# A hybrid decoder layer on one core: x's rows spaced alike, head products in runs of like matmuls, conv halves of 272 columns

## The chip, the core and the metric

One core of a Trainium2 chip runs the whole layer in one launch. TensorE (PE) multiplies: a matmul takes a 128x128 block of weights, which a separate weight load (PEld) brings in, and streams a moving operand of up to 512 columns past it into a bank of PSUM. VectorE (DVE), ScalarE (ACT) and GpSimd (POOL) do elementwise work; SyncE (SP) and POOL issue the transfers between device memory and the on-chip memory SBUF (128 partitions). The metric is the time of one execution on the device in microseconds (us).

## The reference

One layer, 512 tokens after 16 meta tokens (L = 528), model width 2048, 8 attention heads of 128, 1024 conv channels, feed-forward width 5632.

```python
h = concat([meta, x])                                  # 528 x 2048
p = rmsnorm(h, g_mix) @ w_in
q, k, v, gb, gc, u = split(p)                          # 1024 columns each
q, k = rmsnorm(q per head), rmsnorm(k per head)
o_attn = stick_breaking_attention(q, k, v)             # sigmoid gates, reverse cumulative sum of logs
o_conv = gb * causal_dwconv3(gc * u, conv_w)           # y_t = sum of w[i] * (gc*u)_{t-2+i}
o = concat([rmsnorm(o_attn), rmsnorm(o_conv)])
h = h + o @ w_out
h = h + (silu(n2 @ w_gate) * (n2 @ w_up)) @ w_down     # n2 = rmsnorm(h, g_ffn)
return h[16:]
```

## The kernel before

Everything is kept transposed: channels on the partitions, tokens along the free dimension. A product in near-fp32 precision is made of three matmuls per 128 channels of the contraction: a value is split into a high and a low part (`split`: ACT copies the high part, DVE subtracts it), and weights high x data high, weights high x data low, weights low x data high are summed in PSUM. Weights come in quads of eight 128x128 blocks: SP loads a quad into `w_buf` (line 172), ACT and DVE split it into `s_buf` (lines 188 and 189), two or three quads ahead of PE.

x, scaled by its gain, is held as sixteen pairs of tiles `nh0`..`nh15` (high) and `nl0`..`nl15` (low), one pair for each 128 of the 2048 channels (`split_x`). Each tile is 528 floats long, 2112 bytes of a partition, and they lie one behind the other. The list of them is `n_hl`.

The order of the work, stage by stage:

- **Start** (0 to 30 us): x arrives tile by tile; the products for k and q of head 0 (`pk0`, `pq0`) advance together in groups of 2, 2, 4, 4 and 4 tiles of x, as ACT and DVE split them.
- **Heads** (to about 345 us): for each head a product for k (`pk`), q (`pq`) and v (`pv`), `product_steps` (lines 271 to 287). k and v have 528 columns and are done in two parts of 264, one in each of two PSUM banks; for a tile of x the two parts follow each other for each of the three kinds (L280, L282, L284). q has the 512 real tokens in one part. The attention of the head before is woven in: `after(n, work)` queues a piece of work, and `tick()`, called once for each tile of x, issues it after n ticks. Attention's own matmuls are the few on lines 465 to 616.
- **First two conv channel blocks** (345 to about 415 us): products `pcu` (c and u, 520 columns in two parts of 260 that begin at token column `C0` = 8) and `pb` (b, 512 columns in one part).
- **Other six conv channel blocks** (415 to about 604 us): Winograd's form of Strassen's product, seven block products for eight (`pair_product`, `block_product`, lines 730 to 785). Its operands are halves of x's columns of width `CH` = 260, and sums of them: parts of `n_hl`, and three sums in `blk`. `form_blocks(k)` makes the sums of tiles k and k+8 during the heads: SP loads four quarters of x (`x4`), ACT scales them, DVE makes the sums, both split them, and SP stores them to `fc` in device memory. Later POOL loads three of the four kinds into `blk` (line 701) and the fourth over x's own second halves (line 708). For two channel blocks at a time `pair` is called three times: c and u of each, then b of both.
- **Output projection** (604 to 786 us, `po`), **gate and up** (786 to 1606 us, moving operands `f0`..`f6`), **down** (to the end, `first` and `ring`). In the last two every moving operand is 256 columns wide and its rows lie 1024 bytes apart; the tiles are made with `slots`, which begins each one 16 bytes into its space and pads it by 240 bytes more. In `po` the rows are 512 columns, 2048 bytes apart. None of this is touched by the change.

The tile framework orders each engine's instructions by a schedule that it computes when the program is built, and each engine runs its own in order.

Of the kernel before, what the change touches and what calls it, by code (L numbers as in the profile page):

```python
# [15 lines left out]
P = 128  # L16
D = 2048
# [16 lines left out]
def hybrid_layer(ctx: ExitStack, tc: tile.TileContext, xT, w_in, w_out, w_gu, w_down, vecs, out):  # L34
# [23 lines left out]
    sm = open_pool("sm", 4, space=PSUM)  # L58

# [211 lines left out]
    def product_steps(parts, acts, n):  # L271

        k, last = 0, n - 1
        while k <= last:
            hi, lo, m = next_w()
            for j in range(m):
                wh, wl = hi[:, j * P : (j + 1) * P], lo[:, j * P : (j + 1) * P]
                ah, al = acts[k]
                for ps, a, b in parts:
                    pe.matmul(ps, wh, ah[:, a:b], start=k == 0, stop=False)  # L280
                for ps, a, b in parts:
                    pe.matmul(ps, wh, al[:, a:b], start=False, stop=False)  # L282
                for ps, a, b in parts:
                    pe.matmul(ps, wl, ah[:, a:b], start=False, stop=k == last)  # L284
                k += 1
                tick()
            yield
# [34 lines left out]
    H = L // 2  # L322
    n_hl = []
# [6 lines left out]
    def x_scale():  # L330
        ve.tensor_tensor(acc, acc, accs[1], ALU.add)
        for a in (0, H):
            ps = small(f"ssx{a}")
            pe.matmul(ps[:, :H], ones, acc[:, a : a + H], start=True, stop=True)
            ve.tensor_scalar(ms[:, a : a + H], ps[:, :H], 1.0 / D, EPS, ALU.mult, ALU.add)
# [11 lines left out]
    def split_x(k):  # L347
        nh = npool.tile([P, L], F32R, tag=f"nh{k}", name=f"nh{k}")
        nl = npool.tile([P, L], F32R, tag=f"nl{k}", name=f"nl{k}")
        g = g_mix[:, k : k + 1]  # L350
        sc.activation(nh, xts[k], AF.Copy, scale=g)
        ve.scalar_tensor_tensor(nl, xts[k], g, nh.bitcast(F32), ALU.mult, ALU.subtract)
        n_hl.append((nh, nl))

    def square_x(k):
# [6 lines left out]

    pk0 = pp.tile([P, 2, 512], F32, tag="pp", name="pk0")
    pq0 = pp.tile([P, 2, 512], F32, tag="pp", name="pq0")
    steps = [
        product_steps([(pk0[:, 0, :H], 0, H), (pk0[:, 1, :H], H, L)], n_hl, KT),
        product_steps([(pq0[:, 0, :], META, L)], n_hl, KT),
# [43 lines left out]
    C0, CH = 8, (L - 8) // 2  # L411
    fc = dram.tile([P, 4, 2, 8, CH], F32R, name="fc")

    def form_blocks(k):

        x4 = stage.tile([P, 4, CH], F32, tag="x4", name=f"x4_{k}")
        st = stage.tile([P, 8 * CH], F32R, tag="st", name=f"st4_{k}").rearrange("p (i a t) -> p i a t", i=4, a=2)
        for i, kk in ((0, k), (2, k + 8)):
            nc.sync.dma_start(x4[:, i : i + 2], two(xT[kk][:, C0:]))
# [20 lines left out]
    def halves(ps, n):  # L440
        return ps[:, :, :n]

# [3 lines left out]
    def qk_norm(ps, g, cols, dst, parts_of, name):  # L446
# [9 lines left out]
        raw_v, s_v = (raw, s) if cols == SEQ else (two(raw), two(s))  # L456
        sc.activation(s_v, ps, AF.Square)
        sc.activation(raw_v, ps, AF.Copy, scale=g)
# [21 lines left out]
    def head(h):  # L480

        if h:
            pk = pp.tile([P, 2, 512], F32, tag="pp", name=f"pk{h}")
            product([(pk[:, 0, :H], 0, H), (pk[:, 1, :H], H, L)], n_hl)
        else:
            pk = pk0
# [3 lines left out]
        after(8 if h else 11, qk_norm(halves(pk, H), g_k, L, kn[:, :L], (kh, kl, 384), f"k{h}"))  # L490

        if h:
            pq = pp.tile([P, 2, 512], F32, tag="pp", name=f"pq{h}")
            product([(pq[:, 0, :], META, L)], n_hl)
        else:
            pq = pq0
# [3 lines left out]
        after(9 if h else 12, qk_norm(pq[:, 0, :], gq_s, SEQ, qn, (qh, ql, SEQ), f"q{h}"))  # L500

        pv = pp.tile([P, 2, 512], F32, tag="pp", name=f"pv{h}")
        product([(pv[:, 0, :H], 0, H), (pv[:, 1, :H], H, L)], n_hl)
        vt = t512(L, "e", 2)
        ve.tensor_tensor(two(vt[:, :L]), halves(pv, H), two(r), ALU.mult)
# [120 lines left out]
    for h in range(HEADS):  # L626
        if h > 1:
            after(6, lambda h=h: form_blocks(h - 2))
        head(h)
# [23 lines left out]
    def conv_taps(j, c1, c2, y):  # L653

        ve.tensor_tensor(c1, c1, two(r2[:, C0:]), ALU.mult)
        ve.tensor_tensor(c1, c2, c1, ALU.mult)
        cu = c1.rearrange("p a b -> p (a b)")
        o = META - 2 - C0
        sc.activation(y, cu[:, o : o + SEQ], AF.Copy, scale=cw[:, 3 * j : 3 * j + 1])
        for t in (1, 2):  # L660
            ve.scalar_tensor_tensor(
                y, cu[:, o + t : o + t + SEQ], cw[:, 3 * j + t : 3 * j + t + 1], y, ALU.mult, ALU.add
            )
# [12 lines left out]
    for j in range(CONV_FIRST):  # L676
        if j == 0:
            after(2, lambda: form_blocks(6))
            after(12, lambda: form_blocks(7))
        c1, c2 = halves_of("e"), halves_of("e2")  # L680
        for c in (c1, c2):
            p = pp.tile([P, 2, 512], F32, tag="pp", name="pcu")
            product([(p[:, 0, :CH], C0, C0 + CH), (p[:, 1, :CH], C0 + CH, L)], n_hl)
            sc.copy(two(c), halves(p, CH))
# [3 lines left out]
        product([(pb[:, 0, :], META, L)], n_hl)  # L688
        gb = t512(SEQ, "e2", 2)[:, :SEQ]
        sc.copy(gb, pb[:, 0, :])  # L690
        if j == 0:
# [6 lines left out]
            blk = blk_pool.tile([P, 3, 2, 8, CH], F32R, name="blk")  # L698
            for i, n in enumerate((3, 0, 2)):
                for part in range(2):  # L700
                    gp.dma_start(blk[:, i, part], fc[:, n, part], max_dma_last_dim=4160)
# [4 lines left out]
    for k in range(8):  # L706
        for part in range(2):
            gp.dma_start(n_hl[k][part][:, C0 + CH :], fc[:, 1, part, k])

    def parts_of(kk, a):  # L710
        return lambda part, k: n_hl[kk + k][part][:, a : a + CH]

    def of_blk(i):
        return lambda part, k: blk[:, i, part, k]

    conv_acts = [
        parts_of(0, C0), of_blk(0), of_blk(1), of_blk(2), parts_of(0, C0 + CH), parts_of(8, C0), parts_of(8, C0 + CH)
# [69 lines left out]
    def pair(acts):  # L787
        c1, c2 = halves_of("e"), halves_of("e2")
# [4 lines left out]
    for j in range(CONV_FIRST, HEADS, 2):  # L793
        ys = []
        for m in range(2):
            c1, c2 = pair(conv_acts)
# [17 lines left out]
        for m in range(2):  # L814
            s = t512(SEQ, "e", 2)[:, :SEQ] if j == HEADS - 2 else cpool.tile([P, SEQ], F32, tag="s", name=f"sq{j}_{m}")
            with tc.high_priority(1 << 20) if j == HEADS - 2 else ExitStack():
                conv_out(j + m, gbs[m][:, META - C0 :], ys[m], slots[m][:, 0], slots[m][:, 1], s, ve)
# [43 lines left out]

    def pad(pool, n):
        pool.tile([P, n // 4], F32, name=f"pad_{pool.name}")
# [372 lines left out]
```

## Time and profile before

| | |
|---|---|
| median of 3 runs | 2040.07 us (2039.51 to 2040.22) |
| the profiled execution: its own time | 2039.67 us |
| its span, from first to last instruction | 2038.0 us |
| DVE busy | 1718.7 us (84%) |
| ACT busy | 1049.0 us (51%) |
| POOL busy | 379.9 us (19%) |
| DMA queue of SP / of POOL | 229.51 MB, 35.5% / 129.65 MB, 24.2% of 16 engines' span |

A row of the timeline gives the start in us, how long it took, the engine, the line, the operation, output<-inputs, partitions x columns, and a count where rows were merged. TensorE's matmuls overlap: the next one begins long before the one before has left the array, so what counts for the time is the distance from start to start, called pitch below, and not the duration in the row.

### The profile page before, as it was taken

Reading aid. Unit: us, or ns where it says so; the run is one execution under the profiler, and the core shown is the slowest. Engines: PE = TensorE matmul, PEld = TensorE weight load, DVE = VectorE, ACT = ScalarE, POOL = GpSimd, SP = SyncE. Lnnn points to the kernel's source line nnn. Section 1 sums busy time; section 2 is a strip of 40 time slices with the busy share of each in tenths; the row PEclk is TensorE's granted clock in tenths of the full one; section 3 lists DMA queues with packets and bytes.
Section 4 is the critical chain, followed back from the end, with each engine's and each line's share of the span. In section 5 each row is a group of like instructions: output and inputs, shape, how many; then the busy total and the mean of one; then the engine's idle time right before and its main releaser. Section 6 shows DMA issues by size and latency. Waiting matters only on the chain.

```text
span 2038.0 us, 39734 instructions
## 1 busy us (share of the span) xinstructions
PE 2028.5 (100%) x16158; PEld 1964.8 (96%) x16158; DVE 1718.7 (84%) x2202; ACT 1049.0 (51%) x1517; POOL 379.9 (19%) x532
## 2 busy tenths in 40 slices
PE   9999999999999999999999999999999999999999
PEld 8999999999998889999999999999999999999999
DVE  8788878588877678998988988988989988888887
ACT  7666666344443435554554554555555544444443
POOL 0111111210015440101111111110110252222111
PEclk9999999999999999999999999999999999999999
DMA  6333344753365656556555555555555999989864
GB/s 231 111 119 124 124 136 130 253 150 104 104 212 181 187 175 231 155 169 174 159 165 158 159 161 161 158 161 158 163 160 155 278 312 310 243 236 262 228 154 89
DMA packets 161863, 361.70 MB, mean 177 GB/s; under 512 B 13584, under 2 KB 73488, under 8 KB 161680
## 3 DMA queue, kind: packets, MB, share of 16 engines
q1 hardware_dynamic: 79744, 229.51, 35.5%
q0 software_dynamic: 81936, 129.65, 24.2%
q8 instruction: 127, 2.08, 0.4%
q14 instruction: 56, 0.46, 0.1%
HBM read 278.50 MB, written 80.61 MB: 176 GB/s over the span
## 4 chain that ended last, share of the span: by engine, by line
PE 93%; DVE 3%; ACT 2%; issue 1%; DMA 1%; POOL 0%; DVEq 0%; POOLq 0%; ACTq 0%
PE x L742 13%; PE x L744 13%; PE x L743 13%; PE z L742 6%; PE z L743 6%; PE z L744 6%; PE y L742 3%; PE y L743 3%; PE y L744 3%; PE po L843 3%; PE po L845 3%; PE po L844 3%; PE pv L280 2%; PE pv L284 1%; PE pv L282 1%
## 5 line engine op out<-in xcount | busy, mean ns | idle before, releaser
L188 ACT CAST s_buf<-w_buf 128x1024 fp32r<-128x1024 f32 (+2 forms) x665 | 659.3, 991 | 764.7 <-PE x L743 341.1
L189 DVE TENSOR_TENSOR s_buf<-w_buf,s_buf 128x1024 fp32r<-128x1024 f32 (+2 forms) x665 | 767.2, 1154 | 174.4 <-ACT s_buf L188 174.1
L742 PE MATMUL x<-f,s_buf 128*128 128x256 f32 x1408 | 387.7, 275 | 0.6 <-ACT sides L772 0.5
L744 PE MATMUL x<-f,s_buf 128*128 128x256 f32 x1408 | 387.2, 275 | 0.0
L743 PE MATMUL x<-f,s_buf 128*128 128x256 f32 x1408 | 387.2, 275 | 0.0
L201 DVE TENSOR_TENSOR w_buf<-w_buf 128x1024 f32<-128x1024 f32 (+1 forms) x243 | 277.5, 1142 | 14.7 <-DMA w_buf<-w_in 10.4
L742 PEld LDWEIGHTS x<-f,s_buf 128*128 128x128 f32 x1408 | 264.3, 188 | 1.4 <-ACT sides L772 0.9
L743 PEld LDWEIGHTS x<-f,s_buf 128*128 128x128 f32 x1408 | 264.3, 188 | 0.0
L744 PEld LDWEIGHTS x<-f,s_buf 128*128 128x128 f32 x1408 | 264.3, 188 | 0.0
L1038 POOL DMA_DIRECT2D fd<-s x147 | 103.6, 921 | 705.0 <-DVE s L295 703.7
L742 PE MATMUL z<-f,s_buf 128*128 128x256 f32 x704 | 193.6, 275 | 0.0
L743 PE MATMUL z<-f,s_buf 128*128 128x256 f32 x704 | 193.6, 275 | 0.0
L744 PE MATMUL z<-f,s_buf 128*128 128x256 f32 x704 | 193.6, 275 | 0.0
L744 PE MATMUL x<-ring,s_buf 128*128 128x256 f32 x608 | 167.3, 275 | 1.0 <-DVE s_buf L189 1.0
L742 PE MATMUL x<-ring,s_buf 128*128 128x256 f32 x608 | 167.2, 275 | 0.0
L743 PE MATMUL x<-ring,s_buf 128*128 128x256 f32 x608 | 167.2, 275 | 0.0
L742 PEld LDWEIGHTS z<-f,s_buf 128*128 128x128 f32 x704 | 132.1, 188 | 0.0
L744 PEld LDWEIGHTS z<-f,s_buf 128*128 128x128 f32 x704 | 132.1, 188 | 0.0
L743 PEld LDWEIGHTS z<-f,s_buf 128*128 128x128 f32 x704 | 132.1, 188 | 0.0
L1108 POOL DMA_DIRECT2D out_T<-d x62 | 60.2, 1001 | 302.7 <-DVE d L1116 232.3
L744 PEld LDWEIGHTS x<-ring,s_buf 128*128 128x128 f32 x608 | 114.1, 188 | 1.2 <-DVE s_buf L189 1.2
L742 PEld LDWEIGHTS x<-ring,s_buf 128*128 128x128 f32 x608 | 114.1, 188 | 0.0
(379 smaller groups left out, 5252.3 us busy)
## 6 DMA issues: line engine op xcount, KB each, us to landing
w_buf<-w_gu SPq DMA_DIRECT2D x176, 512.0 KB, 3.4
w_buf<-w_in SPq DMA_DIRECT2D x92, 512.0 KB, 3.4
fd<-s POOLq DMA_DIRECT2D x147, 256.0 KB, 5.2
w_buf<-w_down SPq DMA_DIRECT2D x96, 384.0 KB, 4.9
ring<-fd POOLq DMA_DIRECT2D x42, 768.0 KB, 8.7
w_buf<-w_out SPq DMA_DIRECT2D x32, 512.0 KB, 3.6
out_T<-d POOLq DMA_DIRECT2D x62, 256.0 KB, 5.4
fc<-st SPq DMA_DIRECT2D x8, 1040.0 KB, 6.2
```

Source lines behind the costliest of these rows:

```text
L188: sc.copy(hi, src)
L189: in_turn(ve.tensor_tensor(lo, src, hi.bitcast(F32), ALU.subtract), turn)
L201: in_turn(ve.tensor_tensor(sums[name], a, b, ALU.add), turn)
L280: pe.matmul(ps, wh, ah[:, a:b], start=k == 0, stop=False)
L742: pe.matmul(p, hi[:, kk], act(0, k), start=start and j == k == 0, stop=False, skip_group_check=skip)
L743: pe.matmul(p, hi[:, kk], act(1, k), start=False, stop=False, skip_group_check=skip)
L744: pe.matmul(p, lo[:, kk], act(0, k), start=False, stop=k == n - 1, skip_group_check=skip)
L843: pe.matmul(ps, hi[:, kk], ah, start=k == order[0], stop=False)
L844: pe.matmul(ps, hi[:, kk], al, start=False, stop=False)
L845: pe.matmul(ps, lo[:, kk], ah, start=False, stop=k == order[-1])
L1038: gp.dma_start(fd[c][s][:, :, k], t[:, :, i])
L1108: gp.dma_start(two(out[j]), c, accum_op=ALU.add)
```

## The change

It has five pieces.

1. The high and low part of a tile of x become one tile `n{k}` of 2 x 576 floats; the low part lies 2304 bytes behind the high one, and the next tile 4608 bytes further. Both distances are multiples of 256 bytes. The used row begins 12 floats in and may be 544 long (528 are x's).
2. `product_steps` turns its loops: the parts are now outside and the eight tiles of a quad inside, and a part's three kinds of matmul stay together. `H` becomes 272 (META + 256), so 528 columns are 272 + 256; q and b, 512 columns in one part before, become 256 + 256. `row_of` places the two parts one behind the other across the border of two PSUM banks.
3. The conv's halves `CH` become 272 columns wide, from token column 0 and from 256; the two halves overlap by 16 columns. The pair for b needs only 256 (`last_of` takes the last 256 of each half). `blk` gets rows of 288 floats, so that POOL's load into it has pieces of 272 floats (1088 bytes) where two long ones of 1040 floats were.
4. x's quarters for `form_blocks` are loaded by a `load_x4` of its own, queued at another tick, and in four transfers of 272 columns for two of 520.
5. The descriptor space of POOL's transfers is halved (`dynamic_dma_scratch_size=8192`), which makes room for the longer rows. The square in `conv_out` is written over b's buffer where a tile of its own was.

```diff
-            for j in range(m):
+            for i, ((ps, a, b), j) in enumerate((part, j) for part in parts for j in range(m)):
                 wh, wl = hi[:, j * P : (j + 1) * P], lo[:, j * P : (j + 1) * P]
-                ah, al = acts[k]
-                for ps, a, b in parts:
-                    pe.matmul(ps, wh, ah[:, a:b], start=k == 0, stop=False)
-                for ps, a, b in parts:
-                    pe.matmul(ps, wh, al[:, a:b], start=False, stop=False)
-                for ps, a, b in parts:
-                    pe.matmul(ps, wl, ah[:, a:b], start=False, stop=k == last)
-                k += 1
-                tick()
+                ah, al = acts[k + j]
+                pe.matmul(ps, wh, ah[:, a:b], start=k + j == 0, stop=False)
+                pe.matmul(ps, wh, al[:, a:b], start=False, stop=False)
+                pe.matmul(ps, wl, ah[:, a:b], start=False, stop=k + j == last)
+                if i % len(parts) == len(parts) - 1:
+                    tick()
+            k += m
...
-    H = L // 2
+    H, ROW = META + T2, 2304 // 4
...
-        nh = npool.tile([P, L], F32R, tag=f"nh{k}", name=f"nh{k}")
-        nl = npool.tile([P, L], F32R, tag=f"nl{k}", name=f"nl{k}")
+        n = npool.tile([P, 2 * ROW], F32R, tag=f"n{k}", name=f"n{k}")
+        n_row = n.rearrange("p (a t) -> p a t", a=2)[:, :, 12 : 12 + 2 * H]
+        nh, nl = (n_row[:, i, :L] for i in range(2))
...
+    def row_of(ps, a=0):
+        flat = ps.rearrange("p a b -> p (a b)")[:, 512 - H + a :]
+        return flat[:, : L - a], [(flat[:, : H - a], a, H), (flat[:, H - a : L - a], H, L)]
...
-    C0, CH = 8, (L - 8) // 2
+    CH = H
...
+    def load_x4(k):
+        blk_x[k] = x4 = stage.tile([P, 4, CH], F32, tag="x4", name=f"x4_{k}")
+        for i, kk in ((0, k), (2, k + 8)):
+            for m in range(2):
+                nc.sync.dma_start(x4[:, i + m], xT[kk][:, m * T2 : m * T2 + CH])
...
-            blk = blk_pool.tile([P, 3, 2, 8, CH], F32R, name="blk")
+            blk = blk_pool.tile([P, 8 + 48 * 288], F32R, name="blk")
+            blk = blk[:, 4 : 4 + 48 * 288].rearrange("p (i k a t) -> p i k a t", i=3, k=8, a=2)
...
-                    gp.dma_start(blk[:, i, part], fc[:, n, part], max_dma_last_dim=4160)
+                    gp.dma_start(blk[:, i, :, part, :CH], fc[:, n, part])
...
-        gbs = pair(conv_acts)
+        gbs = pair([last_of(act) for act in conv_acts], T2)
...
-    nc = bacc.Bacc("TRN2", target_bir_lowering=False, num_devices=1)
+    nc = bacc.Bacc("TRN2", target_bir_lowering=False, num_devices=1, dynamic_dma_scratch_size=8192)
```

TensorE in head 3's product for k, before (each row with x2 is the two parts):

```order
L280 MATMUL pk3_1569<-nh0_170,s_buf_112 128x264 x2
L282 MATMUL pk3_1569<-nl0_171,s_buf_112 128x264 x2
L284 MATMUL pk3_1569<-nh0_170,s_buf_112 128x264 x2
L280 MATMUL pk3_1569<-nh1_174,s_buf_112 128x264 x2
L282 MATMUL pk3_1569<-nl1_175,s_buf_112 128x264 x2
```

The same place now, the end of the first part and the beginning of the second (the number behind `n` is the tile of x, 0 to 15):

```order
L283 MATMUL pk3_1704<-n6_248,s_buf_112 128x272
L284 MATMUL pk3_1704<-n6_248,s_buf_112 128x272
L282 MATMUL pk3_1704<-n7_251,s_buf_112 128x272
L283 MATMUL pk3_1704<-n7_251,s_buf_112 128x272
L284 MATMUL pk3_1704<-n7_251,s_buf_112 128x272
L282 MATMUL pk3_1704<-n0_170,s_buf_112 128x256
L283 MATMUL pk3_1704<-n0_170,s_buf_112 128x256
```

Twenty-four matmuls of 272 columns go through the quad's eight tiles of x, and then twenty-four of 256 go through the same eight tiles again.

TensorE at the start, the first rows behind the warm-up, before (`pk0` and `pq0` are head 0's k and q):

```order
L280 MATMUL pk0_124<-nh0_170,s_buf_112 128x264 x2
L280 MATMUL pq0_125<-nh0_170,s_buf_112 128x512
L282 MATMUL pk0_124<-nl0_171,s_buf_112 128x264 x2
L284 MATMUL pk0_124<-nh0_170,s_buf_112 128x264 x2
L282 MATMUL pq0_125<-nl0_171,s_buf_112 128x512
L280 MATMUL pk0_124<-nh1_174,s_buf_112 128x264 x2
```

And now:

```order
L282 MATMUL pk0_124<-n0_170,s_buf_112 128x272
L282 MATMUL pq0_125<-n0_170,s_buf_112 128x256
L283 MATMUL pk0_124<-n0_170,s_buf_112 128x272
L284 MATMUL pk0_124<-n0_170,s_buf_112 128x272
L283 MATMUL pq0_125<-n0_170,s_buf_112 128x256
L284 MATMUL pq0_125<-n0_170,s_buf_112 128x256
L282 MATMUL pk0_124<-n1_173,s_buf_112 128x272
```

Half of tile 0's columns are done, and tile 1 is asked for, before the other half of tile 0 is touched.

SP's queue in the heads, where `x4` is loaded, before (`fc<-st` is the store of the sums made before it):

```order
L428 DMA fc_466<-st4_5_3555 1024x1x260
L419 DMA x4_6_3927<-xT 128x520 x2
L172 DMA w_buf_111<-w_in 128x1024 x6
L428 DMA fc_466<-st4_6_3928 1024x1x260
L419 DMA x4_7_4076<-xT 128x520 x2
L172 DMA w_buf_111<-w_in 128x1024 x3
L428 DMA fc_466<-st4_7_4077 1024x1x260
```

And now:

```order
L443 DMA fc_498<-st4_5_3889 1024x1x272
L429 DMA x4_6_4029<-xT 128x272 x4
L175 DMA w_buf_111<-w_in 128x1024 x6
L443 DMA fc_498<-st4_6_4312 1024x1x272
L429 DMA x4_7_4431<-xT 128x272 x4
L175 DMA w_buf_111<-w_in 128x1024 x2
L443 DMA fc_498<-st4_7_4463 1024x1x272
```

Between the stores the loads of x stand where they stood, right behind the store before; they are four for two, and the last store has passed one load of weights.

More of the change, by code (lines that the diff above doesn't have):

```diff
@@ L682, in hybrid_layer @@
             p = pp.tile([P, 2, 512], F32, tag="pp", name="pcu")
-            product([(p[:, 0, :CH], C0, C0 + CH), (p[:, 1, :CH], C0 + CH, L)], n_hl)
-            sc.copy(two(c), halves(p, CH))
+            row, parts = row_of(p)
+            product(parts, n_hl)
+            for m in range(2):
+                sc.copy(two(c)[:, m], row[:, m * T2 : m * T2 + CH])
         y = t512(SEQ, "v", 2)[:, :SEQ]
@@ L785, in pair_product, with pair @@
         return x
-    def pair(acts):
-        c1, c2 = halves_of("e"), halves_of("e2")
+    def pair(acts, n):
+        c1, c2 = (halves_of(t)[:, : 2 * n] for t in ("e", "e2"))
         x = pair_product(acts, two(c1), two(c2), sides)
```

78 lines of the change are left out of this document (42 added, 36 removed).

## The prediction, made before the run

> **What bounds the kernel now.** The page's busy times and its chain of waits come first.
>
> ```profile
> PE 2028.5 (100%) x16158; PEld 1964.8 (96%) x16158; DVE 1718.7 (84%) x2202; ACT 1049.0 (51%) x1517; POOL 379.9 (19%) x532
> PE 93%; DVE 3%; ACT 2%; issue 1%; DMA 1%; POOL 0%; DVEq 0%; POOLq 0%; ACTq 0%
> ```
>
> TensorE is busy throughout and is 93% of the chain, so the time is a sum of matmul pitches and a few waits. The page's "mean ns of one" can't give pitches, since matmuls overlap; a count of matmuls in a stretch without waits can. Three such stretches, from the window view (stretch, length, then busy time and count of PE, PEld, DVE, ACT and POOL, granted clock, DMA share and GB/s), and behind them the groups by shape that give one matmul's duration (the ns between the bars):
>
> ```profile
> 440.00:480.00 40.00, 40.00 (x337) 40.00 (x336) 34.99 (x39) 18.86 (x25) 0.00 (x0) 1.00 0.34 106
> 900.00:980.00 80.00, 80.00 (x708) 80.00 (x708) 72.02 (x81) 41.27 (x54) 14.46 (x21) 1.00 0.61 174
> 660.00:740.00 80.00, 80.00 (x355) 66.24 (x354) 55.56 (x77) 31.81 (x51) 36.19 (x40) 1.00 0.60 180
> L742 PE MATMUL x<-nh,s_buf 128*128 128x260 f32 x216 | 61.0, 283 | 0.5 <-ACT sides_c L772 0.5
> L744 PE MATMUL x<-f,s_buf 128*128 128x256 f32 x1408 | 387.2, 275 | 0.0
> L843 PE MATMUL po<-oa,s_buf 128*128 128x512 f32 x128 | 49.8, 389 | 0.0
> ```
>
> A count takes in matmuls that had begun before the stretch: at 283, 275 and 389 ns each and the pitches that follow, about 2.4, 2.4 and 1.7 of them.
>
> - 440 to 480, the conv's pairs, 260 columns: 40 us / 334.6 = **119.5 ns**, 0.460 ns a column.
> - 900 to 980, gate and up, 256 columns: 80 / 705.6 = **113.4 ns**, 0.443 a column.
> - 660 to 740, output projection, 512 columns: 80 / 353.3 = **226.4 ns**, 0.442 a column.
>
> Four columns more cost 6.1 ns in the first, where 0.443 each makes 1.8. So 260 columns pay 4.4 ns that 256 and 512 don't. The clock is granted in full (1.00) in all three, and DVE is busier beside the second (72.02 of 80 us) than beside the first (34.99 of 40), so neither is the reason. What differs is in the code: in the second and third every moving row begins a multiple of 256 bytes behind the last one; in the first no two neighbours do. The heads' rows, from the timeline of head 3, tell size from spacing:
>
> ```profile
> 139.87 0.40 PE L280 MATMUL pk<-nh,s_buf 128*128 128x264 f32 x2
> ...
> 142.53 0.40 PE L284 MATMUL pk<-nh,s_buf 128*128 128x264 f32 x2
> 142.76 0.39 PE L280 MATMUL pq<-nh,s_buf 128*128 128x512 f32 x1
> ...
> 145.30 0.40 PE L284 MATMUL pq<-nh,s_buf 128*128 128x512 f32 x1
> ```
>
> From 139.87 to 142.76 are 24 matmuls of 264, 120.4 ns each, 3.5 over the rate of 0.443. From 142.76 to 145.30 are 11 of 512, **230.9 ns** each where `po` has 226.4: the same size, 4.5 ns dearer, and q's rows lie 2112 bytes apart, 64 off a multiple of 256. So about 4 ns a matmul go with the spacing of the rows, whatever the size.
>
> **The change part by part.** Its own count of matmuls comes from the groups by shape, of which one row each stands here (each has two or five sisters of like count):
>
> ```profile
> L280 PE MATMUL pv<-nh,s_buf 128*128 128x264 f32 x256 | 53.0, 288 | 0.2 <-ACT tmp L458 0.2
> L280 PE MATMUL pq<-nh,s_buf 128*128 128x512 f32 x128 | 50.3, 393 | 0.0
> L280 PE MATMUL pcu<-nh,s_buf 128*128 128x260 f32 x128 | 25.8, 283 | 0.0
> L280 PE MATMUL pb<-nh,s_buf 128*128 128x512 f32 x32 | 12.7, 397 | 0.0
> ```
>
> k and v: six groups of 256 are 768 pairs of 264. q and b: 3 x 128 + 3 x 32 = 480. c and u: 3 x 128 / 2 = 192 pairs of 260. Conv pairs: 3 rounds x 3 calls x 7 products x 24 = 1512 of 260.
>
> The unknown is the pitch of 272 columns in a run. Its ends: 0.443 x 272 = 120.4 ns, if it runs as 256 and 512 do where rows are spaced alike; or what 272 columns cost now, in attention's few:
>
> ```profile
> 134.66 0.28 PE L527 MATMUL z<-qh,kh 128*128 128x272 f32 x1
> 134.78 0.29 PE L528 MATMUL z<-ql,kh 128*128 128x272 f32 x1
> 134.90 0.29 PE L529 MATMUL z<-qh,kl 128*128 128x272 f32 x1
> 135.03 0.41 PE L532 MATMUL z<-qn,kn 128*128 128x144 f32 x2
> ```
>
> That is (135.03 - 134.66) / 3 = 123.3 ns, 2.9 dearer. I take 120.4: in the new heads all 24 rows of a run begin a multiple of 256 apart (2304 and 4608 bytes), as in the 256-column run of 900 to 980, which has the same weights buffer and the same three kinds per tile; in attention weights and rows change tiles at each step.
>
> 1. k and v: a pair goes from 2 x 120.4 = 240.8 to 120.4 + 113.4 = 233.8. 768 x -7.0 = **-5.4 us**.
> 2. q and b: 230.9 to 2 x 113.4 = 226.8. 480 x -4.1 = **-2.0 us**.
> 3. c and u: 2 x 119.5 = 239.0 (528 columns for 520 now) to 233.8. 192 x -5.2 = **-1.0 us**.
> 4. Conv pairs: two calls of three take 272 columns, 1008 x (120.4 - 119.5) = +0.9 us; b's takes 256, 504 x (113.4 - 119.5) = -3.1 us. In `blk` (three products of seven, 648 matmuls) the low row lies 1152 bytes behind the high one, 128 off a multiple of 256, so two steps of three aren't alike: 432 x 4.4 (the surplus of 260 above) = +1.9 us. Bounds 0 and 648 x 4.4 = 2.9. Together **-0.3 us**.
> 5. Start. The new order asks for the low half of x's tile 7 after 10 matmuls of 272 and 10 of 256 of its group, 2.3 us, where the old one came to it after 20 of 264 and 10 of 512, 4.7 us. DVE makes that half between 16.17 and 16.93 (the first of three merged), and TensorE used it at 17.37:
>
> ```profile
> 16.17 2.12 DVE L352 SCALAR_TENSOR_TENSOR nl<-xt,vec,nh 128x528 fp32r<-128x528 f32 x3
> 17.37 0.40 PE L282 MATMUL pk<-nl,s_buf 128*128 128x264 f32 x2
> ```
>
> So there is 0.44 us of slack for 2.4 us of haste: up to +2.0 us of wait here, less what the earlier waits of the same kind have already delayed. The schedule moves ACT's squares behind the next splits, which helps. Queued behind a wait is the rest of the group and then all of TensorE. I take **+1.0 us**, between 0 and +2.0.
>
> 6. The loads of x for `form_blocks` don't move on SP's queue, as the rows of its order show. The only wait at stake is 0.8 us on TensorE where the first conv product meets head 7's attention (0.3 us before the first of these rows and 0.5 between the two, beyond a pitch):
>
> ```profile
> 364.37 0.41 PE L284 MATMUL pcu<-nh,s_buf 128*128 128x260 f32 x2
> 364.94 0.49 PE L587 MATMUL c<-sph,carry 128*128 128x512 f32 x1 [0.17 <-ACT sph L294]
> 365.65 0.50 PE L588 MATMUL c<-spl,carry 128*128 128x512 f32 x1 [0.22 <-DVE spl L295]
> ```
>
> That waits for ACT and DVE, not for a transfer. I take 0, with 0.8 either way. DVE's and ACT's wider sums (272 for 260 columns, 5%) lie beside matmuls; if that cover goes, DVE's extra is some 1 us in the heads.
>
> 7. `blk` in shorter pieces. Before, six transfers were issued and landed so:
>
> ```profile
> L701 POOL DMA_DIRECT2D blk<-fc x6: 723/733/752, 379.9 to 383.5; - x6
> DMA to landing us min/median/max: 5.8/13.1/20.9
> 390.00:395.00 5.00, 5.00 (x43) 5.00 (x43) 3.75 (x6) 1.54 (x2) 0.00 (x0) 1.00 1.10 409
> 405.00:410.00 5.00, 5.00 (x23) 4.09 (x22) 2.97 (x3) 0.00 (x0) 4.29 (x9) 1.00 1.14 280
> 410.00:415.00 5.00, 5.00 (x28) 4.25 (x27) 2.64 (x3) 2.64 (x4) 3.06 (x6) 1.00 1.14 232
> ```
>
> From 390 to 395 the engines move pieces of 4160 bytes at 409 GB/s; from 405 to 415, saturated too, pieces of 1040 bytes (L708) beside a load of weights at 280 and 232. The last of the six landed at 383.5 + 20.9 = 404.4. `blk` is 6.7 MB now; with some 2 MB of weights beside it at 232 to 280 GB/s that is 31 to 38 us from 380, until 411 to 418, and the loads over x's second halves, some 2 MB on the same queue, come behind. They are wanted by the fifth and sixth products of the first pair:
>
> ```profile
> 413.99 0.28 PE L742 MATMUL y<-nh,s_buf 128*128 128x260 f32 x1
> ```
>
> With 24 matmuls a product these begin 11.5 and 14.3 us after 413.99, and all of that some 7 us sooner by steps 1 to 5: 418 and 421. So the third of `blk` just makes it and the loads behind it may not: between 0 and +6 us. TensorE's whole queue stands behind such a wait. I take **+1.0 us**, near the end of no wait, since before `blk` was in time by 21 us (425.5 less 404.4). The halved descriptor space isn't exercised by any row; POOL is 19% busy, and what it loads for TensorE later is asked for long ahead. I take 0.
>
> Sum: -5.4 - 2.0 - 1.0 - 0.3 + 1.0 + 1.0 = **-6.7 us**. The profiled execution took 2039.67 us (1.7 more than its span), 0.4 below the median of 2040.07; that becomes 2033.0 us, and by the median 2033.4. I forecast **2033 us**.
>
> **The rivals.** (a) **272 columns stay irregular.** 272 x 4 is 64 bytes off a multiple of 256, so a row ends where the next doesn't begin. Attention's 123.3 speaks for it. 960 in the heads and 576 of the conv outside `blk` at +2.9 are +4.5 us: 2037.5.
>
> (b) **Spacing is not the cause; a matmul pays a fixed amount and its columns.** Then halving q and b costs 480 x 4 = +1.9 us, c and u +192 x 8 x 0.443 = +0.7, the wider conv 1008 x 12 x 0.443 = +5.4, b's -504 x 4 x 0.443 = -0.9; with +2.0 for steps 5 and 7, +9.1: **2049**, slower. It decides at the heads' 256 columns: 117 ns or more is this rival. Against it are the stretches with no fixed amount at all (226.4 is twice 113.4).
> The Trainium skill, TensorE: Matmul & The Clock Gate, section "Back-to-back issue gap", has such a rule: columns / 2.4 plus 2.5 ns. By its figures the same edits would be about +6 us, an estimate. By that rule 260 columns are 1.7 ns dearer than 256; the trace has 6.1, and 113.4 where the rule has 109.2, so here the measurement speaks against it.
>
> (c) **A late transfer or a longer start** at the upper ends of steps 5 and 7 takes back 3 to 6 us more of the gain: 2036 to 2039. For it: the narrow margins there. Against it: ACT and DVE are ordered anew at the start, and 232 GB/s may not be the engines' limit for such pieces.
>
> **How the numbers follow.** Forecast 0.48 (2029 to 2036), (a) 0.22, (b) 0.13, (c) 0.17. A measurement of this kernel can tell about 0.2%, 4.1 us, from no change. Faster by more (below 2036.0): nearly all of the forecast, a quarter of (a), a third of (c): 0.58. Within: the rest of (a) and (c): 0.27. Slower (above 2044.2): (b) and a little of (c): 0.15. The lower bound takes every free term at its best (no cost in `blk`, none in steps 5 and 7, the wait in 6 gone: -4.7 together), 2028; the upper one reaches through (a) and (c), which may meet, and short of (b): 2044.
>
> **What would show it.** In the new profile: the 272-column runs of `pk` and `pv` at 120 ns (272 irregular: 123 and up); the 256-column runs at 113 (b: 117); `pq` as two such runs; the conv's `blk` products dearer than those on `n` by some 3 ns a matmul; the conv's first pair without a wait for a transfer. Such a wait, on `blk` or on x's second halves 10 to 15 us into that pair, or on POOL's queue later, would speak for (c). The forecast is wrong as a whole if 256 columns in the heads don't come at 113.

## The result, and the profile after

| | before | after |
|---|---|---|
| median | 2040.14 us (2039.51 to 2041.67, 4 runs) | 2053.32 us (2050.95 to 2054.99, 4 runs) |
| the profiled execution, its span | 2039.67, 2038.0 us | 2054.32, 2052.6 us |

The changed kernel takes 1.0062 times as long, 95% interval 1.0049 to 1.0075: 13 us slower, where 7 us less was forecast and the range ended at 2044.

The page of the changed kernel, busy times and chain:

```profile
PE 2033.6 (99%) x16638; PEld 1989.1 (97%) x16638; DVE 1719.2 (84%) x2210; ACT 1053.2 (51%) x1521; POOL 383.7 (19%) x532
PE 87%; DVE 5%; ACT 3%; DMA 2%; issue 1%; SPq 1%; POOL 1%; ACTq 0%; DVEq 0%
```

TensorE's share of the chain fell from 93% to 87%, and VectorE, ScalarE and transfers took the rest: there are new waits. TensorE's waits, by the view that adds them up (who waited, for what, us in all, times, the longest one), in the changed kernel:

```profile
PE c L600 <- DVE spl L296: 5.4, 7, 1.0
PE po L866 <- DMA oc<-od_c: 1.8, 2, 1.0
...
PE c L599 <- ACT sph L295: 0.9, 1, 0.9
PE ss_k L477 <- DVE sl_k L296: 0.9, 3, 0.4
```

and what stood there before:

```profile
PE c L588 <- DVE spl L295: 0.5, 2, 0.3
...
PE c L587 <- ACT sph L294: 0.2, 1, 0.2
```

The same two waits of attention grew from 0.7 to 6.3 us. Each stage's length, from its first matmul in the timeline to the next stage's first (a second profile of the changed kernel stands beside the first, from the run changed_again below):

| us | before | after | after, again |
|---|---|---|---|
| start, to the first product for v | 30.04 | 32.18 | 34.05 |
| heads | 307.88 | 315.36 | 314.17 |
| c, u, b of two channels | 76.07 | 76.49 | 76.35 |
| six conv channels in pairs | 182.60 | 184.80 | 184.56 |
| output projection | 178.71 | 181.87 | 178.70 |
| the rest | 1262.67 | 1261.92 | 1261.90 |

Of the first profile's 14.65 us the heads lost 7.5, the output projection 3.2 (not in the second profile), the pairs 2.2, the start 2.1 (4.0 in the second). By the same lengths the heads end at 338, the pairs begin at 414 and end at 597, and the output projection ends at 775 us before the change: the 345, 604 and 786 in the list of stages above are 7 to 11 us late.

**The pitches.** A product for v in the changed kernel, the first rows of its 272-column and of its 256-column run and two later rows of the latter (start, duration, count at the end):

```profile
159.42 0.29 PE L282 MATMUL pv<-n,s_buf 128*128 128x272 f32 x1
...
162.46 0.28 PE L282 MATMUL pv<-n,s_buf 128*128 128x256 f32 x1
...
163.40 0.28 PE L284 MATMUL pv<-n,s_buf 128*128 128x256 f32 x1
...
165.10 0.28 PE L284 MATMUL pv<-n,s_buf 128*128 128x256 f32 x1
```

24 matmuls of 272 take 3.04 us, 126.7 ns each, where 120.4 was forecast. The first eight of 256 take 117.5 each, and the next fifteen 113.3: a run of 256 settles at the forecast rate, but only after some six to ten. Means over all matmuls, taken from the starts with gaps of over 60 ns left out: 272 columns 124.9 in the heads and in the pairs, 256 columns 115.0 for k and v and 114.7 for q, and in the pairs 115.4 on x's rows and 117.8 on `blk`. Other rules for what is left out move these means by up to 0.3 ns.

**The waits.** Attention works through a head's three blocks of keys from the last to the first. Between two blocks a row is carried over: VectorE adds it (`lw<-c,sp`), ScalarE makes its high part (`sph`), VectorE its low part (`spl`), and six ticks of product matmuls later TensorE needs both (`c<-sph`, `c<-spl`). VectorE in head 3 before:

```profile
153.42 0.55 DVE L593 TENSOR_TENSOR lw<-c,sp 1x400 f32<-1x400 f32 x1
153.90 0.55 DVE L596 TENSOR_TENSOR lb<-lb,c 128x400 f32<-128x400 f32 x1
154.38 0.41 DVE L426 SCALAR_TENSOR_TENSOR x<-x 128x260 f32<-128x260 f32 x1
154.72 0.68 DVE L295 TENSOR_TENSOR spl<-lw,sph 1x512 fp32r<-1x512 f32 x1
```

and after:

```profile
156.15 0.56 DVE L605 TENSOR_TENSOR lw<-c,sp 1x400 f32<-1x400 f32 x1
156.64 0.69 DVE L304 TENSOR_TENSOR tmp<-tmp 128x528 f32<-128x528 f32 x1
157.25 0.55 DVE L608 TENSOR_TENSOR lb<-lb,c 128x400 f32<-128x400 f32 x1
157.74 0.69 DVE L305 TENSOR_TENSOR tmp<-tmp,tmp 128x528 f32<-128x528 f32 x1
158.35 0.67 DVE L296 TENSOR_TENSOR spl<-lw,sph 1x512 fp32r<-1x512 f32 x1
```

Two wide steps of the norm of k (L304, L305) now stand ahead of `spl`, where one narrow step for the conv's sums stood. TensorE at the two places, before and after:

```profile
155.34 0.40 PE L587 MATMUL c<-sph,carry 128*128 128x512 f32 x1
155.58 0.39 PE L588 MATMUL c<-spl,carry 128*128 128x512 f32 x1
```

```profile
157.71 0.40 PE L599 MATMUL c<-sph,carry 128*128 128x512 f32 x1
159.08 0.50 PE L600 MATMUL c<-spl,carry 128*128 128x512 f32 x1 [0.98 <-DVE spl L296]
```

Before, `spl` ended at 154.72 + 0.68 = 155.40 and was used at 155.58: 0.2 us of slack (at the same place in the other heads it was 0.05 to 0.4). After, it ended at 159.02, and TensorE's whole queue stood. The second new delay, the store of the block sums, the loads of x behind it on SyncE, and ScalarE's first use of x; before:

```profile
133.34 0.53 SPq L428 DMA_DIRECT2D fc<-st  x1
133.91 1.29 SPq L419 DMA_DIRECT2D x<-xT  x2
...
140.25 0.73 ACT L421 ACTIVATE x<-x,vec 128x520 f32<-128x520 f32 x1 [0.45 <-DMA x<-xT]
```

and after:

```profile
136.29 0.52 SPq L443 DMA_DIRECT2D fc<-st  x1
136.87 4.14 SPq L429 DMA_DIRECT2D x<-xT  x4
...
143.43 0.75 ACT L436 ACTIVATE x<-x,vec 128x544 f32<-128x544 f32 x1 [1.41 <-DMA x<-xT]
```

Head 3 begins at 128.53 before and 130.72 after, so x is used 11.7 us into the head before and 12.7 after: the loads moved to `load_x4` did not come sooner, they came 1.0 us later, since the store ahead of them did (0.8); and issuing the four behind it took 4.14 us, where the two took 1.29. Over the heads ScalarE waited 10.1 us for x in seven waits, where it was 2.8 in six. Behind ScalarE's wait stand attention's `sph` and the squares of k (`ss_k`).

### The profile page after: what moved, and what is told of

The parts are those of the page before. It is cut to its first block, busy times and chain, and to the rows that moved or that the text cites. A ratio compares the mean times of both kernels' runs of the same rounds, so it can differ in the third digit from the quotient of the medians.

```text
span 2052.6 us, 40751 instructions
## 1 busy us (share of the span) xinstructions
PE 2033.6 (99%) x16638; PEld 1989.1 (97%) x16638; DVE 1719.2 (84%) x2210; ACT 1053.2 (51%) x1521; POOL 383.7 (19%) x532
## 4 chain that ended last, share of the span: by engine, by line
PE 87%; DVE 5%; ACT 3%; DMA 2%; issue 1%; SPq 1%; POOL 1%; ACTq 0%; DVEq 0%
PE x L767 13%; PE x L765 13%; PE x L766 13%; PE z L766 7%; PE z L767 7%; PE z L765 7%; PE y L766 3%; PE y L767 3%; PE y L765 3%; PE po L866 3%; PE po L868 3%; PE po L867 3%; DVE s_buf L192 1%; PE pv L282 1%; PE pv L284 1%
```

## The experiments

The theory after the comparison: the loss in the heads is **waits, not pitches**, from two links that feed each other (VectorE's order around the carried row, and x behind the store), and the pitches didn't fall because alike spaced rows are not what makes matmuls regular. The rival for the first: the engines are simply too full now, and a wait removed comes back elsewhere. The rival for the second: the spacing is right, and 272 is one odd size.

**carry_soon**: the carried row at high priority in the schedule.

```diff
-                ve.tensor_tensor(lw[0:1, b0 - n : b0], c[0:1, :n], sp[0:1, a : a + n], ALU.add)
-                split(th[0:1, :], tl[0:1, :], lw[0:1, a0:b0])
+                with tc.high_priority(1 << 20):
+                    ve.tensor_tensor(lw[0:1, b0 - n : b0], c[0:1, :n], sp[0:1, a : a + n], ALU.add)
+                    split(th[0:1, :], tl[0:1, :], lw[0:1, a0:b0])
```

> The changed kernel, but VectorE and ScalarE take the three instructions that carry a head's running sum from one block to the next (one add of a 1x400 row, its split) as soon as they can; in the changed kernel two 128x528 steps of the norm of k stand between the add and the split's second half, in the old one two shorter ones. Theory A (the order on VectorE makes TensorE wait 0.5 to 1.15 us in front of the second 512-column matmul of each head's last sums, seven times, 6.7 us in all): one 0.7 us step leaves that gap, the waits fall to about 0.5 each and the time to 2049 us. Theory B (VectorE is behind anyway, whoever goes first): the wait comes back in front of the next head's norm of k (L476 to L477) and the time stays at 2053.

2044.22 us (2042.78 to 2046.30), ratio to the kernel before 1.0020 (1.0011 to 1.0029). VectorE at the same place in its timeline:

```profile
155.62 0.56 DVE L606 TENSOR_TENSOR lw<-c,sp 1x400 f32<-1x400 f32 x1
156.10 0.69 DVE L304 TENSOR_TENSOR tmp<-tmp 128x528 f32<-128x528 f32 x1
156.72 0.55 DVE L609 TENSOR_TENSOR lb<-lb,c 128x400 f32<-128x400 f32 x1
157.20 0.67 DVE L296 TENSOR_TENSOR spl<-lw,sph 1x512 fp32r<-1x512 f32 x1
```

One step of 0.69 us left the gap, and 9.1 us left the time, twice what A had: the waits for `spl` fell from 5.4 to 0.9 us, and the heads took 309.46 us for 315.36. B is out. (The heads give 5.9 us and the c, u, b stage 1.1 in the two profiled executions; the rest of the 9.1 can't be placed, since the output projection's 3.2 stand in the first profile alone.)

**x_before_store**: the four loads of x are issued ahead of the store of the sums made before.

```diff
     def load_x4(k):
...
                 nc.sync.dma_start(x4[:, i + m], xT[kk][:, m * T2 : m * T2 + CH])
+        store_sums()
...
-        nc.sync.dma_start(fc[:, :, :, k].bitcast(F32), st.bitcast(F32))
+        sums_st.append((k, st))
+        if k == 7:
+            store_sums()
```

> The changed kernel, but SyncE issues the four loads of x for the next block sums ahead of the 1088 KB store of the last ones, not behind it. Theory A (the loads wait behind the store, ScalarE stands 1.41 us for them in each head, and with it the squares of k that TensorE waits for 0.25 to 0.6 us): ScalarE's wait for x is gone, the waits for sl_k of 2 us in all are gone, and the waits for the carried sum shrink somewhat: 2050 us. Theory B (the late loads lie beside slack, and only the order on VectorE matters): ScalarE's wait goes, TensorE's waits stay, 2053 us.

2043.13 us (2042.02 to 2044.75), ratio 1.0014 (1.0005 to 1.0023). ScalarE no longer waits for x in the heads, and issuing the four loads took 1.75 us for 4.14; TensorE's waits for the carried row, in the same view as above:

```profile
PE c L608 <- DVE spl L296: 0.7, 4, 0.2
```

VectorE's order is still the changed one here (both wide steps ahead of `spl`), and yet the heads took 308.10 us. Ten us by a cure that leaves the order alone, nine by one that leaves the loads alone: more than A had in both cases. The reading that fits: the order makes the chain long, the late x makes it start late, and at this size the wait needed both.

**cured**: both cures together.

> The changed kernel with both cures (the carried sum as soon as can be, x ahead of the store), the start as changed. Theory A (the two cures break one loop of lateness, each by itself gave 9 to 10 us of it): together hardly more than one, 2041 to 2042, and cured_old_start (2038.85) is better by the start, 2 to 3 us. Theory B (two independent losses): 2053.3 - 9.1 - 10.2 = 2034.

2040.33 us (2039.49 to 2042.70), ratio 1.0002 (0.9993 to 1.0011). The two gains are not independent (that would have been 2034): together 13.0 us, not 19.3. The heads took 305.78 us, 2.1 less than before the change: 1.4 of it by the pitches (below), the rest by waits that the old kernel had too (0.7 us for `sph` and `spl`).

**old_nesting**: the loops of `product_steps` turned back, everything else as changed.

```diff
-            for i, ((ps, a, b), j) in enumerate((part, j) for part in parts for j in range(m)):
+            for j in range(m):
...
+                for ps, a, b in parts:
+                    pe.matmul(ps, wh, ah[:, a:b], start=k == 0, stop=False)
...
```

> The changed kernel with the old loops: for a tile of x the two parts (272 and 256 columns) follow each other for each of the three kinds. Rows, widths, conv and loads as changed. Theory A (turning the loops changed the order on VectorE and the start, and gained little in the pitches, 240.2 ns for a pair against 241.4): the order on VectorE around the carried sum is the old one again, the waits there go (-7 us), the first product for v begins about 2 us sooner, pairs cost 241 to 242: 2045 us. Theory B (the waits come from the later loads of x, whatever the loops): 2052 us or more.

2041.98 us (2041.25 to 2042.57), ratio 1.0007 (0.9998 to 1.0016). VectorE's order in heads 1 to 6 is the old one again (`lb` and one narrow step ahead of `spl`), and its waits in the view:

```profile
PE ss_k L479 <- DVE sl_k L298: 0.7, 2, 0.4
...
PE c L602 <- DVE spl L298: 0.6, 3, 0.2
```

So it was the turning of the loops that reordered VectorE: the schedule is computed from all instructions, and other matmuls in another order gave another one. The start is back too (29.81 us). A pair of 272 and 256 in turn cost 123.8 + 117.0 = 240.8 ns, so the runs' 240.0 were worth 0.6 us in all.

**runs_of_264**: both cures, and the heads, c, u and b cut at 264 (`h = L // 2` in `row_of`), still in runs.

> The changed kernel with both cures for its waits (the carried sum as soon as can be, and x loaded ahead of the store), and with heads, c, u and b of the first two channels cut at 264 in place of 272: runs of 264 and 264 columns for k, v, c and u, of 248 and 264 for q and b. The conv's halves stay at 272. Theory A (in a run on alike spaced rows every size goes at 0.443 ns a column, and only 272 is odd): 264 costs 116.9, 248 costs 109.8; a pair 233.8 for 240.2, 960 pairs, 6 us less than the cured kernel, about 2037. Theory B (any size that isn't 256 or 512 pays 3 to 5 ns wherever its rows lie): 264 costs 120 to 121 and 248 about 113, nothing gained, about 2043.

2086.81 us (2084.18 to 2087.69), ratio 1.0225 (1.0211 to 1.0239), which neither theory had. The pitches follow B: 264 cost 121.4 ns, 248 cost 113.4 (its share would be 109.8). The time is the waits' and the clock's. VectorE in head 2 of this kernel

```profile
129.44 0.71 DVE L305 TENSOR_TENSOR tmp<-tmp,tmp 128x528 f32<-128x528 f32 x1
130.19 0.43 DVE L306 TENSOR_SCALAR tmp<-tmp 128x528 f32<-128x528 f32 x1
130.66 0.71 DVE L307 TENSOR_TENSOR tmp<-tmp,tmp 128x528 f32<-128x528 f32 x1
131.40 0.71 DVE L492 TENSOR_TENSOR kn<-tmp,tmp 128x528 f32<-128x528 f32 x1
132.03 0.55 DVE L615 TENSOR_TENSOR lw<-c,sp 1x400 f32<-1x400 f32 x1
```

does the whole norm ahead of the carried row, and TensorE waits for ScalarE's `sph` behind it:

```profile
PE c L608 <- ACT sph L295: 15.3, 6, 2.7
```

The first product for v waits another 5.7 us, and behind these waits the clock granted to TensorE falls to half, as here (the granted clock is the third number from the end):

```profile
180.19:183.60 3.41, 3.41 (x16) 3.31 (x17) 2.31 (x3) 3.21 (x6) 0.56 (x2) 0.50 0.00 0
```

There are 27 us of such stretches from 36 to 372 us, with TensorE busy for 24 of them, which is some 12 us lost (an estimate: half of the busy time). Eight columns moved from one part to the other turned the order once more, and by far more than the pitches are worth.

**rows_alone**: the kernel before with the new row spacing (and the halved descriptor space) alone.

```diff
-        nh = npool.tile([P, L], F32R, tag=f"nh{k}", name=f"nh{k}")
-        nl = npool.tile([P, L], F32R, tag=f"nl{k}", name=f"nl{k}")
+        n = npool.tile([P, 2 * ROW], F32R, tag=f"n{k}", name=f"n{k}")
+        nh, nl = (n.rearrange("p (a t) -> p a t", a=2)[:, i, 12 : 12 + L] for i in range(2))
```

> The kernel before with one thing changed: the high and low part of a tile of x lie 2304 bytes apart in one tile of 4608, so that every row begins a multiple of 256 bytes behind the last one (and POOL's descriptor space is halved, as in the change, to make the room). Loops, parts of 264, 512 and 260 columns, conv and loads as before. Theory A (the prediction's: the spacing is the cause of the surplus, whatever the size): 264 columns cost 116.9 ns for 120.7, 512 cost 226.4 for 230.7, 260 on x's rows about 115 for 119.7; 1536 x 3.8 + 480 x 4.3 + 384 x 4.5 + 864 x 4.5 = 13 us less, about 2027. Theory B (alike spaced rows help 512 and 256 columns alone): 480 x 4.3 = 2.1 us less, 2038; 264 stays at 120 to 121 and 260 near 119.7. Neither has new waits, since the order on the other engines is the old one.

2040.20 us (median of 11 runs, 2038.73 to 2041.60 but for one of 2076.03), ratio 1.0000 (0.9991 to 1.0009). Neither theory: 264 columns cost 120.7 ns, as before, and so do 260 (119.7) and 512. q in its timeline, eleven matmuls apart:

```profile
184.80 0.40 PE L280 MATMUL pq<-n,s_buf 128*128 128x512 f32 x1
...
187.34 0.40 PE L284 MATMUL pq<-n,s_buf 128*128 128x512 f32 x1
```

2.54 us / 11 = 230.9 ns. Rows that begin alike modulo 256 bytes are **not enough**. It also shows that the halved descriptor space costs nothing that can be told.

**rows_at_128**: the same, with the rows begun at another place (`48 : 48 + L` for `12 : 12 + L`).

> rows_alone with x's rows begun 144 bytes further into their space, so that the 512-column rows of q and b begin at the remainder 128 modulo 256 where the output projection's rows begin (in rows_alone at 240); nothing else differs. Theory A (the start within 256 bytes decides whether 512 columns go at 226.4 or 230.4): q and b at 226.4, 1.9 us less than rows_alone, 2038.3. Theory B (the distance from row to row decides, 2048 and 4096 in the output projection against 2304 and 4608 here, or the work between): 230 still, 2040.2.

2039.84 us (2038.87 to 2041.55), ratio 0.9997 (0.9988 to 1.0006), which the time can't tell from rows_alone. The timeline can:

```profile
184.66 0.40 PE L280 MATMUL pq<-n,s_buf 128*128 128x512 f32 x1
...
186.06 0.39 PE L280 MATMUL pq<-n,s_buf 128*128 128x512 f32 x1
...
187.19 0.39 PE L284 MATMUL pq<-n,s_buf 128*128 128x512 f32 x1
```

Six at 233.3 ns, then five at 226.0: here 512 columns settle at the output projection's rate, and at the other start they never do. That is A's mechanism; over all matmuls the means are 228.9 (q) and 227.8 (b) for 230.4, because attention breaks the run again and again, and that makes 0.8 us, not 1.9.

**nested_conv_260**: old_nesting with the conv's halves 260 wide, from token columns 12 and 268 (`C0, CH = 12, 260`, and the slices that go with it).

> old_nesting (2042.0 us) with the conv's halves 260 wide, not 272: they begin at token columns 12 and 268, 256 apart, so b's pair still takes 256 columns; rows of the three sums in blk stay at 1152 bytes. Theory A (260 costs what it cost before, 119.7, and 272 costs 124.9): 1008 x 5.2 = 5.2 us less, 2036.8. Theory B (on alike spaced rows 260 goes at 0.443 a column, 115.1): 576 of the 1008 gain 9.8 and the rest 5.2, 7.9 us less, 2034. If the widths cost their share of columns alone (12 x 0.443 = 5.3 ns), A's number too; the pitch in the trace tells them apart.

2038.36 us (median of 11 runs, 2037.33 to 2039.10 but for one of 7241.65, which nothing on record explains), ratio 0.9990 (0.9981 to 0.9999). 260 cost 120.0 on `blk` and 120.5 on x's rows, which are spaced alike: A, and B is out. The pairs took 180.11 us for 184.64, 4.5 less; the heads lost 1.8 of that in this kernel's order.

**cured_old_start**: both cures, and in the start alone a tile of x at a time, both parts, before the next tile. Within a tile a part's three kinds stay together, which in the old loops they did not.

> The changed kernel with both cures (carried sum soon, x ahead of the store) and with the old loops in the start alone (a tile of x at a time for head 0's k and q); the later products keep their runs. Theory A (the start's term of the prediction was too small: runs over a group of tiles ask for the last tile's low half too soon, and cost 2 to 3.6 us): the first product of v begins at 30 us, and with the two cures the time is 2040 us. Theory B (the longer start comes from ACT's and VectorE's order, not from TensorE's): v begins at 32 to 34 us still, and the time is that of the cures together, 2042 to 2043.

2038.85 us (2038.05 to 2040.41), ratio 0.9993 (0.9984 to 1.0002). v began at 31.19 us, against 32.09 in cured: 0.9 us less, and 1.5 by the medians. Not all of it came back (old_nesting, with the old loops throughout, began at 29.81); what holds the rest was not tried.

**oc_first**: POOL's loads for the output projection in the order in which they are used.

```diff
-                    gp.dma_start(t, od[name])
+                    tc.stamp_issue_order_token(gp.dma_start(t, od[name]).ins, "o_loads")
```

> The changed kernel, but POOL loads the two first conv channel blocks of the output projection (oc) ahead of the attention's eight (oa), not between the fourth and the fifth. Theory A (TensorE waits 1.1 and 1.0 us for these two, and the clock granted to it falls behind the waits, about 3.9 us in all): no wait, the clock stays at 1.0 there, 2049.4 us. Theory B (the transfers are limited together, so a wait for oa takes its place some 8 us later): about 2052. If the wait was an accident of the one profiled execution: 2053.

2053.07 us (2051.95 to 2053.97), ratio 1.0062 (1.0048 to 1.0076): no gain. The wait for oc is gone from its profile, and this one has come:

```profile
PE po L866 <- DMA oa<-od_a: 0.7, 1, 0.7
```

**changed_again**: the changed kernel, unchanged.

> The changed kernel once more, for a second profile. In the first one the stretch from the output projection's first matmul to gate and up's first took 181.87 us (178.71 before), with waits of 1.1 and 1.0 us for oc and a lower granted clock behind them; oc_first took 179.73 there without a better median. Theory A (the wait belongs to the kernel): the same waits, 181 to 182 us. Theory B (an accident of how transfers fell in that execution): under 180, and the waits per head (1.15 us for the carried sum, 0.25 to 0.6 for sl_k) as in the first profile.

2051.45 us, one run. No wait for oc, 178.70 us for the stage; `spl` again 5.4 us in seven waits. So the 3.2 us there don't come in every execution. The margin is thin, though: among the other profiles cured has one such wait of 1.2 us and cured_old_start two of 1.8 in all, and the kernel before has none. The start took 34.05 us here, with a lower clock in it (step 5 below).

**cured_old_start_260**: cured_old_start with the halves of 260.

> cured_old_start (2038.85 us) with the conv's halves 260 wide, from token columns 12 and 268. By the pitches of nested_conv_260 (120.0 to 120.5 for 124.7, 1008 matmuls): 4.4 us less, 2034.4, which is 0.28% faster than the kernel before. If the order on the other engines turns again with the narrower sums: 2038 to 2040.

2035.21 us (2034.88 to 2035.89, 8 runs), ratio **0.9975** (0.9965 to 0.9985): 5.3 us faster than the kernel before, near the 2034.4 expected. This version beats both.

## Why the prediction was wrong

Point by point, by its own steps; the pitches are means as above.

| step | forecast | measured |
|---|---|---|
| 1 k and v, a pair | 240.8 to 233.8, -5.4 | 241.4 to 240.0, -1.1 |
| 2 q and b | 230.9 to 226.8, -2.0 | 230.7 to 229.4 (q), 230.1 to 227.6 (b), -0.7 |
| 3 c and u, a pair | 239.0 to 233.8, -1.0 | 240.2 to 239.6, -0.1 |
| 4 conv pairs | -0.3 | +2.2 |
| 5 start | +1.0, up to 2.0 | +2.1; +4.0 in the second profile, at a lower clock |
| 6 loads of x, other engines' order | 0, 0.8 either way | +8 to +9 |
| 7 `blk` in shorter pieces | +1.0 | 0 |

Steps 1 to 4 were to gain 8.7 us and lost 0.3; steps 5 and 6 make up most of the 13.

- **The step that failed first** is the sentence "So about 4 ns a matmul go with the spacing of the rows, whatever the size." It was read off a comparison of stages that differ in more than spacing, and rows_alone refutes it. What the runs put in its place: alike spaced rows are not enough; a run settles at 0.443 ns a column or not, by its size and by where its rows begin. By the addresses in the built programs, 256 columns settled with rows at 240 modulo 256 bytes, 512 at 128 and not at 240, and 248, 260, 264 and 272 at none of the places tried (not every size was tried at 128 and at 240). For 256 columns the place matters too, and the changed kernel shows it by itself. The fifth of the seven products in b's pairs reads the sums loaded over x's second halves, in rows spaced like the rest but begun at 48 modulo 256; the sixth and seventh are back at 240. The first row of each:

```profile
477.63 0.28 PE L765 MATMUL x<-n,s_buf 128*128 128x256 f32 x1
...
480.48 0.28 PE L765 MATMUL y<-n,s_buf 128*128 128x256 f32 x1
...
483.22 0.28 PE L765 MATMUL x<-n,s_buf 128*128 128x256 f32 x1
```

Twenty-four at 118.8 ns, never settling, then twenty-four at 114.2 that settle after two. It is the same in all three of b's calls, and in nested_conv_260, where those rows begin at 0. Rival (a) named 272; its 123.3 ns, from attention's few, was still too low (124.9).
- **Step 4** follows from it: 1008 x (124.9 - 119.7) = +5.2 us where +0.9 stood; b's runs gave 288 x 4.3 + 216 x 2.0 = -1.7 where -3.1 stood; gaps of over 60 ns in that stage fell from 1.6 to 0.3 us. Sum +2.2. The sign that `blk`'s products would be dearer than those on x's rows by some 3 ns came at 256 columns (117.8 for 115.4, and for 113.3 once settled) and not at 272 (125.0 for 124.7).
- **The step that cost most** is 6. It looked at SyncE's order, saw that the loads stood where they had stood, and took 0, with VectorE "beside matmuls". The row that it shows at 365.65, with 0.22 us of wait for `spl`, is this very link in head 7; that the other heads had only 0.05 to 0.4 us to spare there was not looked up, and the order of VectorE and ScalarE in the heads was not compared. The sum held nothing there and no rival more than the 0.8 to 1 us of that step, so the range held no such case; the heads' 7.5 and 6.3 us in the two profiles, and the 1.4 that the pitches gave there, make 8 to 9.
- **Step 5**: the mechanism was right (the low halves of x's tiles are asked for sooner; three waits for them, 1.0 us, stand in the new start), its size too small by about 1 us. The second profile's other 1.9 us are mostly the clock's; the stretch from 8 to 12 us in the first and in the second profile of the changed kernel:

```profile
8.00:12.00 4.00, 3.95 (x31) 3.76 (x32) 3.60 (x7) 4.00 (x9) 0.00 (x0) 1.00 1.02 364
8.00:12.00 4.00, 3.70 (x18) 3.49 (x18) 3.09 (x6) 2.77 (x6) 0.00 (x0) 0.57 0.98 329
```

A clock of 0.57 over 4 us is about 1.7 us lost (18 matmuls for 31). The same stretch stands in the profiles of x_before_store and oc_first, so in three of the seven kernels and repeats whose start was turned, and in none of the seven whose start goes a tile at a time. That the new waits at the start bring it on is likely, not shown.
- **Step 7**: `blk` landed 26 us after its first issue (390.26 to 416.58 in the trace), not 31 to 38, and x's second halves by 428.48. No wait.
- **Rival (b)** (2049, a fixed amount per matmul) came close to the time for another reason: by its test, 117 ns for the heads' 256, it is out (115.0, and 113.3 once settled). The Trainium skill, TensorE: Matmul & The Clock Gate, section "Back-to-back issue gap", gives N / 2.4 plus 2.5 ns as the gap of a warm matmul taken by itself, 109.2 for 256, an estimate by that rule; the settled 113.3 speaks against it here.

What stays open: why a run settles. That the rows' begin and the size decide, and how many matmuls settling takes, is shown; the part of the machine behind them isn't.

## What to carry to other kernels

Where a framework orders the engines, a change on one engine is a change of every engine's order: look up, in the old profile, each short chain that TensorE comes back for and its slack (here 0.2 us), and compare the order of the engines in that chain, not only of the engine edited. A pitch that differs between two stages is not a property of the one difference that one has in mind: change that one alone first, as rows_alone does. And a load meant to come sooner must be moved ahead of what stands in front of it in its queue.

## What the hardware did that was not expected

- A run of like matmuls has two rates and changes between them after six to ten matmuls: 117.5 then 113.3 ns (256 columns), 233.3 then 226.0 (512). A run that follows matmuls of another shape mostly begins at the slower one again. Where rows begin within 256 bytes decides whether it settles, for 512 columns (at 128, not at 240) and for 256 (at 240, not at 48 or 0).
- Behind the two waits for oc the granted clock fell (stretch, length, busy PE, PEld, DVE, ACT and POOL with counts, granted clock, DMA share, GB/s):

```profile
618.00:620.00 2.00, 1.43 (x4) 1.14 (x5) 0.51 (x1) 0.31 (x1) 0.00 (x0) 0.69 1.13 418
620.00:622.00 2.00, 2.00 (x6) 1.53 (x5) 1.23 (x1) 0.74 (x1) 0.00 (x0) 0.50 0.62 234
622.00:624.00 2.00, 2.00 (x10) 1.64 (x9) 0.69 (x1) 0.63 (x1) 0.00 (x0) 0.96 0.53 123
```

Two waits of 1 us within 3 cost another 1.7 us at a lower clock (8 matmuls from 618.57 to 622.01, 430 ns each for 226); the waits of 1 us once in a head, 43 us apart, left it at 1.00. In runs_of_264 waits of 2.2 to 2.7 us, one in a head, brought it to 0.50 in five heads of seven. The Trainium skill, TensorE: Matmul & The Clock Gate, section "What's actually happening", has a gate with two states, full and half rate, and windows of about 3.4 us: the 0.50 agrees, and so does the 3.4 us that it lasted (by the three rows). That section has half rate come after an idle window of that length; here waits of 1.8 us in all within three were enough, so in this the measurement differs.
